# A bidirectional encoder layer: the delta rule's block inverses issued at two places of a recurrence step instead of four

## The chip, the cores and the metric

The kernel runs on one core of one Trainium2 chip. The time is device microseconds of one launch. "Before" was run three times; the figure compared is the median. One further execution was recorded by the hardware profiler, and the profile comes from that one.

## What is computed

One layer of a hybrid encoder: 2048 tokens of width 1024, batch 1. Three branches read the same normalised input through one projection: grouped-query attention, a bidirectional gated delta rule, and cross-attention into 256 memory tokens. Their joint output is gated by silu(z), projected, normalised and added to the input. The change concerns the delta rule alone. The reference, cut to it:

```
lower = jnp.where(strict, jnp.einsum('...id,...jd->...ij', k_beta, k) * decay, 0.0)
t_mat = lower + jnp.eye(CHUNK, dtype=lower.dtype)
rhs = jnp.concatenate([v * beta[..., None], k_beta * jnp.exp(g)[..., None]], axis=-1)
sol = lax.linalg.triangular_solve(t_mat, rhs, left_side=True, lower=True, unit_diagonal=True)
u, w = sol[..., :dv], sol[..., dv:]
...
def step(state, inp):
    qc, kc, uc, wc, ac, dc = inp
    v_new = uc - jnp.einsum('...cd,...de->...ce', wc, state)
    o = jnp.einsum('...cd,...de->...ce', qc, state) + jnp.einsum('...ij,...je->...ie', ac, v_new)
    state = state * dc[..., None, None] + jnp.einsum('...cd,...ce->...de', kc, v_new)
    return state, o
```

It runs forward and backward over the sequence for four heads, and the two directions are summed. The chunk length is free for the kernel to choose, since the recurrence gives the same result for any.

## The kernel before

The layer runs in stages: norms and projections, attention queries and keys, the delta rule's short convolution, the preparation of its chunk matrices, the recurrence (`step`, about 900 to 1262 us of the profile), attention, and the output product. In the profile most instructions stand under line 51, where a helper records every operation, so they are told apart by their tiles.

**The recurrence.** The kernel uses chunks of 128 tokens. One call of `step` treats one chunk of both directions (d) for a pair of heads (h), so each product is four 128x128 float32 matmuls; in the profile these are eight, and every tile below holds all four. There are 16 steps for each of the two head pairs (hp), 32 in all. In a step:

- the scaling of k by the decay to the chunk's end, on VectorE (line 1012: `xx<-xx,tail`)
- `ks`: k times the state St (line 1016); VectorE then makes v minus it, in place in `xx` (line 1018)
- `qp`: q times the state (line 1025); ScalarE scales it into `oo` (line 1027)
- `tx`: F, the inverse of the chunk's triangular matrix, times that difference (line 1032); VectorE scales it into `vn` (line 1035)
- `kv`: the scaled k times vn (line 1043), added to the state by VectorE (line 1048)
- `av`: the chunk's own matrix times vn (line 1053), added into `oo`, which goes to memory (lines 1055 and 1063).

From the ninth step of a pair on, `oo` is added to the other direction's result on GpSimd and squared on ScalarE (lines 1065 to 1072).

**The inverse.** `inverse(hp, s)` is a Python generator that builds F for one chunk and stops after each of its pieces. Each `next` issues one:

1. the loads `nt` (in the profile `n<-NI`) and `ft` (inverses of the 32-row diagonal blocks), and ScalarE's copies of `ft` into F and T
2. `zz` (profile: `invz`), 32x32 matmuls, and ScalarE's copy `zs`
3. `to` and `fo` (`invt`, `invf`), 32x32 matmuls, VectorE's copies into T and ScalarE's into F
4. `z2` (`invy`), 64x64 matmuls, and ScalarE's copy `z2s`
5. `f2` (`inv`), 64x64 matmuls, copied into F by ScalarE (line 995) and VectorE (line 996).

A step is given three generators: `inv` of its own chunk, `inv1` of the next, `inv2` of the one after. Piece 1 of `inv2` is issued just ahead of the step (line 1114). In the running loop the step of chunk n then issued piece 4 of n+1 ahead of `tx` (line 1028), piece 2 of n+2 after it (line 1037), piece 5 of n+1 ahead of `av` (line 1050) and piece 3 of n+2 after it (line 1059). The call at line 1019 found `inv` finished, except in the first step.

**Gate products as fill.** `fill(n)` issues the next n matmuls of work that nobody waits for yet: the projection of the gate z (profile: `z<-hT,wparts`, 128x512, float16, 24 of them to a tile). They stand between the products of the recurrence so that TensorE has something to do while VectorE and ScalarE work. `FILL[4]` to `FILL[10]` say how many at each place of a step. What is not issued there is issued after the recurrence (line 1122).

**Order and buffers.** TensorE is pinned in this stage (line 786): it runs in the order of the text. The other engines and the DMA queues are ordered by a scheduler that works out when each instruction would be ready. An engine's or a queue's order is then fixed, and an instruction that waits holds up those behind it. The loads of this stage go out on SyncE's queue (SP): `nt`, `ft` and `xx` have two buffers each, `it` one. The products that a step takes out of PSUM share four banks under one tag ("tp"), taken in the order of the text: `ks`, `tx`, `kv`, `av` and the five of `inverse`; `qp` and z have four others. F has three buffers, T two; `vn`, `zs` and `z2s` have one each.

During the second pair's steps `side()` issues the end work of the first pair (`finish`), one transpose group (`ot`) in every second step.

Of the kernel before, what the change touches and what calls it, by code (L numbers as in the profile page):

```python
# [30 lines left out]
QW = 256  # L31
START = 3
LAG = 5
FILL = (72, 10, 216, 6, 2, 5, 2, 6, 0, 6, 2, 40, 0, 8)


@with_exitstack
def hybrid_layer(ctx: ExitStack, tc: tile.TileContext, t: dict, out, dbg=None):
# [24 lines left out]
    def dma(to, of):  # L63
        if to.dtype == F32R:
            to, of = to.bitcast(F32), of.bitcast(F32)
        Q.dma_start(to, of)
# [141 lines left out]
    def mm_ps(name, shape=(128, 512)):  # L208
        return mm_pool.tile(list(shape), F32, tag=mm_tag[0], name=name, bufs=mm_tag[1])

    def tp_ps(name, shape=(128, 512)):
        return ps1.tile(list(shape), F32, tag="tp", name=name, bufs=4)
# [565 lines left out]
    def fill(n):  # L778

        for _ in range(n):  # L780
            filled[0] += 1
            next(fill_units, None)
# [4 lines left out]

    fill(FILL[0])
    def bulk(name):
        return bp.tile([128, 2, 4, TB], F32, tag=name, name=name)  # L790
# [12 lines left out]
    with tc.tile_pool(name="s3g", bufs=1, side="right") as p:  # L803
# [48 lines left out]

        fill(FILL[11])
        gp = p.tile([128, 8, 3, 32], F32, tag="gp", name="gp")
# [9 lines left out]
        for i in range(2):  # L864
# [3 lines left out]
            A.copy(grow[:, i], pr[0:96])  # L868
        fill(FILL[12])
        V.tensor_tensor(tail, psg[:, 1], ngc, op=ALU.add)  # L870
# [7 lines left out]
    with tc.tile_pool(name="s3a", bufs=1) as sv0:  # L878
        p = rows
        for hp in range(2):  # L880
            for c in range(TB):
# [18 lines left out]
                dma(NI_d[hp, :, c].rearrange("d p n h i -> p d (n h i)"), ni.rearrange("p d n h i -> p d (n h i)"))  # L900
                fill(FILL[1])
        pr_pool.close()
        sv1 = pr_pool.enter_context(tc.tile_pool(name="s3c", bufs=1, side="right"))
        for hp in range(2):
# [20 lines left out]
            for d, ft in enumerate(((rr, ni), (ni, rr))):  # L925
                for n in range(2):
                    for b in range(4):
                        o = 64 * d + 16 * b
                        dma(FT_d[2 * hp:2 * hp + 2, d, n, :, b].rearrange("h c j i -> c h (j i)"), ft[n][o:o + 16].rearrange("c h j i -> c h (j i)"))
            fill(FILL[2])  # L930
        pr_pool.close()


    with tc.tile_pool(name="s3b", bufs=1) as p:
# [63 lines left out]
        def step(hp, s, St, oss, inv, inv1, inv2, side):  # L998

            nm = f"{hp}_{s}"  # L1000
            cc = (s, TB - 1 - s)
            sh = [128, 2, 2, 128]
            F = Fb[(hp * TB + s) % 3]
            xx = p.tile([128, 2, 4, 2, 128], F32, tag="xx", name=f"xx{nm}", bufs=2)
            it = p.tile(sh, F32, tag="it", name=f"it{nm}")
            kT, qT, kk, vv = (xx[:, :, i] for i in range(4))
            for d in range(2):
                dma(xx[:, d], bx_d[hp, cc[d]])
                dma(it[:, d], NI_d[hp, d, cc[d], :, 1])
            each = [(d, h, 2 * hp + h, cc[d]) for d in range(2) for h in range(2)]  # L1010
            for d, h, hh, c in each:
                V.tensor_scalar(kk[:, d, h, :], kk[:, d, h, :], tail[:, d, hh, c:c + 1], None, op0=ALU.mult)
            if s > 0:
                ks = tp_ps(f"ks{nm}", sh)
                for d, h, hh, c in each:
                    T.matmul(ks[:, d, h, :], kT[:, d, h, :], St[:, d, h, :], start=True, stop=True)
                for d, h, hh, c in each:
                    V.scalar_tensor_tensor(vv[:, d, h, :], ks[:, d, h, :], ngam[:, d, hh, c:c + 1], vv[:, d, h, :], op0=ALU.mult, op1=ALU.add)
            next(inv, None)
            fill(FILL[4])  # L1020
            oo = p.tile(sh, F32, tag="oo", name=f"oo{nm}", bufs=2)
            if s > 0:
                qp = mm_ps(f"qp{nm}", sh)
                for d, h, hh, c in each:
                    T.matmul(qp[:, d, h, :], qT[:, d, h, :], St[:, d, h, :], start=True, stop=True)
                for d, h, hh, c in each:
                    A.activation(oo[:, d, h, :], qp[:, d, h, :], AF.Copy, scale=gam[:, d, hh, c:c + 1])
            next(inv1, None)
            fill(FILL[5])
            tx = tp_ps(f"tx{nm}", sh)  # L1030
            for d, h, hh, c in each:
                T.matmul(tx[:, d, h, :], F[:, d, h, :], vv[:, d, h, :], start=True, stop=True)
            vn = p.tile(sh, F32, tag="vn", name=f"vn{nm}")
            for d in range(2):
                V.tensor_tensor(vn[:, d], tx[:, d], beta[:, d, 2 * hp:2 * hp + 2, cc[d]].unsqueeze(2).to_broadcast([128, 2, 128]), op=ALU.mult)
            fill(FILL[6])
            next(inv2, None)
            side()
            fill(FILL[7])
            if s < TB - 1:  # L1040
                kv = tp_ps(f"kv{nm}", sh)
                for d, h, hh, c in each:
                    T.matmul(kv[:, d, h, :], kk[:, d, h, :], vn[:, d, h, :], start=True, stop=True)
                if s == 0:
                    V.tensor_copy(St, kv)
                else:
                    for d, h, hh, c in each:
                        V.scalar_tensor_tensor(St[:, d, h, :], St[:, d, h, :], egl[:, d, hh, c:c + 1], kv[:, d, h, :], op0=ALU.mult, op1=ALU.add)
            fill(FILL[8])
            next(inv1, None)  # L1050
            av = tp_ps(f"av{nm}", sh)
            for d, h, hh, c in each:
                T.matmul(av[:, d, h, :], it[:, d, h, :], vn[:, d, h, :], start=True, stop=True)
            if s > 0:
                V.tensor_tensor(oo, oo, av, op=ALU.add)
            else:
                A.copy(oo, av)
            fill(FILL[9])
            next(inv2, None)
            fill(FILL[10])  # L1060
            if s < TB // 2:
                for d in range(2):
                    dma(O_d[0][hp, cc[d]], oo[:, d])
                return
            oi = p.tile(sh, F32, tag="oi", name=f"oi{nm}")
            for d in range(2):
                dma(oi[:, d], O_d[0][hp, cc[d]])
            G.tensor_tensor(oo, oo, oi, op=ALU.add)
            for d, h, hh, c in each:
                A.activation(oi[:, d, h, :], oo[:, d, h, :], AF.Square, accum_out=oss[:, h, c:c + 1])  # L1070
            for d in range(2):
                dma(O_d[1][hp, cc[d]], oo[:, d])
# [30 lines left out]
            next(invs[n])  # L1103
        fill(30)
        for k in range(3):
            for n in range(2 if k < 2 else 1):
                next(invs[n])
            fill(FILL[3])
        invs += [iter(()), iter(())]
        for n, (hp, s) in enumerate(order):  # L1110
            if s == 0:
                St = p.tile([128, 2, 2, 128], F32, tag="St", name=f"St{hp}")
                oss = p.tile([128, 2, TB], F32, tag="oss", name=f"oss{hp}", bufs=2)
            next(invs[n + 2], None)
            step(hp, s, St, oss, *invs[n:n + 3], lambda: next(done, None))
            if s == TB - 1:
                done = finish(hp, oss)
# [283 lines left out]
    for i in range(len(blocks) + LAG + 1):  # L1401
# [27 lines left out]
        for tb in range(2):  # L1429
            n = i - len(blocks) - 2 * tb - LAG + 4  # L1430
# [146 lines left out]
```

## Time and profile before

| what | value |
|---|---|
| median of 3 runs | 2406.45 us (2404.51 to 2410.85) |
| profiled execution | 2407.9 us, span 2405.8 us |
| granted TensorE clock, mean | 0.993 |
| DMA over the span | 471.58 MB, mean 196 GB/s |
| recurrence, 900 to 1262 us | 32 steps |

The span goes from the first to the last instruction. In the lines of the profile a time is in us from the span's start, followed by the duration of the run of like instructions, the engine, the operation, `out<-in` by the program's names, the shape and the count. PE is TensorE's matmul, PEld its weight load, DVE VectorE, ACT ScalarE, POOL GpSimd, SPq the queue of SyncE that issues loads. A bracket at the end gives the idle time of the engine just before, and what ended it. Starts of matmuls are measured and their ends modelled, so distances between starts say more than durations. In the table of waits a line has who waited, for whom, the sum in us, how often, and the longest.

### The profile page before, as it was taken

To read this page: it belongs to the slowest core of one execution; us is meant where nothing else is said; L and a number is where in the kernel's file an instruction comes from. 1 tells how busy PE (TensorE), PEld (TensorE's weight loads), DVE (VectorE), ACT (ScalarE), POOL (GpSimd) and SP (SyncE) were. 2 spreads that over 40 slices of the span, in tenths; PEclk is the share of its full clock that TensorE was granted. 3 is DMA by queue.
4 is the path that set the end of the run, shared out by engine and by line. 5 is a ranking of instruction groups with operands and counts; after the bars stand their busy time and mean duration, and the time that the engine had idled before them with its cause. 6 is when DMAs were issued, how large, how long until landed. Compare 5 with 4: busy or idle time off the path is not lost. (4 is left out here: it accounts for less than half of the span.)

```text
span 2405.8 us, 42213 instructions
## 1 busy us (share of the span) xinstructions
PE 2308.4 (96%) x15846; PEld 1463.4 (61%) x15846; DVE 1652.5 (69%) x3338; ACT 1297.4 (54%) x2508; POOL 717.7 (30%) x431
## 2 busy tenths in 40 slices
PE   6999999999999989999999999999999999999998
PEld 6888874455554437667674566666666666544443
DVE  7777558899867855555553778777888877355553
ACT  5633436644443145555554888888888788211110
POOL 2146431111210231020121544445444445122110
PEclk9999999999999999999999999999999999999999
DMA  6446555434377476677765999999999999775551
GB/s 229 141 126 146 133 117 171 125 111 127 113 245 253 107 205 206 203 245 218 242 221 197 243 247 240 242 244 239 239 248 244 243 241 228 217 246 186 175 184 53
DMA packets 942124, 471.58 MB, mean 196 GB/s; under 512 B 721952, under 2 KB 889440, under 8 KB 941664
## 3 DMA queue, kind: packets, MB, share of 16 engines
q1 hardware_dynamic: 929472, 425.88, 69.4%
q0 software_dynamic: 12448, 43.00, 5.3%
q8 instruction: 125, 2.05, 0.4%
q14 instruction: 79, 0.65, 0.1%
HBM read 207.59 MB, written 108.10 MB: 131 GB/s over the span
## 5 line engine op out<-in xcount | busy, mean ns | idle before, releaser
L51 PEld LDWEIGHTS <-wparts 128*128 128x128 f16 x3072 | 293.1, 98 | 317.4 <-issue 6.2
L51 POOL TENSOR_TENSOR hla<-Pa,hla 128x1281 f16<-128x1281 f32 x128 | 335.8, 2624 | 343.2 <-DVE hla L51 320.1
L51 DVE TENSOR_REDUCE mxa<-sa 128x1 f32<-128x1024 f32 x256 | 313.2, 1223 | 130.5 <-PE sa L51 128.6
L51 PE MATMUL sa<-K,qa 128*128 128x512 f16 x1536 | 373.0, 379 | 20.7 <-ACT Pa L51 10.0
L51 PE MATMUL z<-hT,wparts 128*128 128x512 f16 x1536 | 374.0, 381 | 5.4 <-POOL wparts L51 4.7
L51 PE MATMUL pva<-PT,V 128*128 128x256 f16 x3072 | 376.4, 273 | 0.0
L51 ACT ACTIVATE Pa<-sa,mxa,misc 128x1024 f32<-128x1024 f32 x256 | 305.8, 1198 | 95.9 <-POOL hla L51 81.2
L51 PEld LDWEIGHTS <-V 128*128 128x128 f16 x3072 | 300.6, 98 | 84.9
L51 PE MATMUL o<-wo,mhl 128*128 128x512 f16 x1416 | 308.0, 380 | 5.6 <-ACT mhl L51 3.4
L51 PE MATMUL b<-hT,wparts 128*128 128x512 f16 x1152 | 257.8, 380 | 0.0
L51 PEld LDWEIGHTS <-mhl 128*128 128x128 f16 x1464 | 143.5, 98 | 179.9 <-ACT mhl L51 3.7
L51 PEld LDWEIGHTS <-hT 128*128 128x128 f16 x2304 | 226.5, 99 | 40.5 <-issue 4.8
L51 ACT CAST hla<-Pa 128x2048 f16<-128x2048 f32 x128 | 243.0, 1898 | 4.3 <-DMA PT<-hla 0.2
L51 PEld LDWEIGHTS <-qa 128*128 128x128 f16 x1536 | 150.0, 98 | 156.2 <-issue 25.8
L51 PE MATMUL q<-wparts,hT 128*128 128x256 f16 x1920 | 215.0, 276 | 8.5 <-DVE t L51 8.4
L51 POOL TENSOR_SCALAR wraw<-wraw,wsc 128x1024 f32<-128x1024 f32 (+1 forms) x22 | 77.3, 3514 | 278.6 <-DVE wy L51 222.9
L77 POOL DMA_DIRECT2D gate<-zg x64 | 35.5, 554 | 415.1 <-DVE zg L51 284.1
L51 ACT CAST mhl<-mr 128x2048 f16<-128x2048 f32 (+1 forms) x16 | 29.1, 1818 | 221.8 <-PE o L51 173.3
L51 DVE SCALAR_TENSOR_TENSOR y<-xb,convw,y 128x512 f32<-128x512 f32 x192 | 145.9, 772 | 2.0
L51 POOL TENSOR_TENSOR mg<-mg 128x1536 f32<-128x1536 f32 (+1 forms) x16 | 54.9, 3431 | 236.6 <-DMA mg<-r 168.3
L51 DVE SCALAR_TENSOR_TENSOR hla<-Pa,hla 128x768 f16<-128x768 f32 x128 | 121.7, 951 | 0.0
L51 DVE TENSOR_TENSOR mhl<-mr,mhl 128x2048 f16<-128x2048 f32 (+1 forms) x16 | 45.2, 2827 | 90.1 <-ACT mhl L51 90.1
(356 smaller groups left out, 3185.6 us busy)
## 6 DMA issues: line engine op xcount, KB each, us to landing
xx<-bx SPq DMA_DIRECT2D x64, 512.0 KB, 5.9
wraw<-in_w_in POOLq DMA_DIRECT2D x42, 512.0 KB, 5.3
wor<-in_w_out SPq DMA_DIRECT2D x32, 512.0 KB, 4.2
gate<-zg POOLq DMA_DIRECT2D x64, 256.0 KB, 3.7
NI<-nit SPq DMA_DIRECT2D x32, 512.0 KB, 3.0
mr<-mix SPq DMA_DIRECT2D x13, 1024.0 KB, 6.0
mg<-r SPq DMA_DIRECT2D x13, 768.0 KB
x<-in_x SPq DMA_DIRECT2D x16, 512.0 KB
```

The costliest lines, as they stand in the source:

```text
L51: ins = f(*args, **kw)
L77: nc.gpsimd.dma_start(to, of)
```

## The change

Within a step the pieces of the inverses stand at two places. Ahead of `tx`: piece 5 of the step's own inverse and piece 3 of the next one's. Between `kv` and `av`: piece 4 of the next one's and piece 2 of the one after. So the call of `inv` moves from ahead of `qp` to behind it, and those of `inv2` from after `tx` and after `av` to between `kv` and `av`; the last piece of an inverse is now issued in the step that uses F, and each piece has the same place in every step. Ahead of the loop the second inverse is advanced by one piece fewer. One gate product moves from after `tx` (FILL[7], 6 to 5) to ahead of it (FILL[5], 5 to 6).

```
-FILL = (72, 10, 216, 6, 2, 5, 2, 6, 0, 6, 2, 40, 0, 8)
+FILL = (72, 10, 216, 6, 2, 6, 2, 5, 0, 6, 2, 40, 0, 8)
...
-            next(inv, None)
             fill(FILL[4])
             oo = p.tile(sh, F32, tag="oo", name=f"oo{nm}", bufs=2)
...
                     A.activation(oo[:, d, h, :], qp[:, d, h, :], AF.Copy, scale=gam[:, d, hh, c:c + 1])
+            next(inv, None)
             next(inv1, None)
             fill(FILL[5])
             tx = tp_ps(f"tx{nm}", sh)
...
             fill(FILL[6])
-            next(inv2, None)
             side()
             fill(FILL[7])
...
             fill(FILL[8])
             next(inv1, None)
+            next(inv2, None)
             av = tp_ps(f"av{nm}", sh)
...
             fill(FILL[9])
-            next(inv2, None)
             fill(FILL[10])
...
         for k in range(3):
-            for n in range(2 if k < 2 else 1):
+            for n in range(1 if k else 2):
                 next(invs[n])
             fill(FILL[3])
```

More of the change, by code (lines that the diff above doesn't have):

```diff
@@ L33 @@
 LAG = 5
-FILL = (72, 10, 216, 6, 2, 5, 2, 6, 0, 6, 2, 40, 0, 8)
+FILL = (72, 10, 216, 6, 2, 6, 2, 5, 0, 6, 2, 40, 0, 8)
 @with_exitstack
@@ L1018, in step @@
                     V.scalar_tensor_tensor(vv[:, d, h, :], ks[:, d, h, :], ngam[:, d, hh, c:c + 1], vv[:, d, h, :], op0=ALU.mult, op1=ALU.add)
-            next(inv, None)
             fill(FILL[4])
@@ L1027, in step @@
                     A.activation(oo[:, d, h, :], qp[:, d, h, :], AF.Copy, scale=gam[:, d, hh, c:c + 1])
+            next(inv, None)
             next(inv1, None)
@@ L1036, in step @@
             fill(FILL[6])
-            next(inv2, None)
             side()
@@ L1050, in step @@
             next(inv1, None)
+            next(inv2, None)
             av = tp_ps(f"av{nm}", sh)
@@ L1058, in step @@
             fill(FILL[9])
-            next(inv2, None)
             fill(FILL[10])
@@ L1105, in hybrid_layer @@
         for k in range(3):
-            for n in range(2 if k < 2 else 1):
+            for n in range(1 if k else 2):
                 next(invs[n])
```

## The prediction, made before the change was run

> **What bounds the kernel now.** I read the page first, then TensorE's timeline through one recurrence step without a wait, then the table of waits between the first and last step, and only then the other engines around the places where TensorE did wait.
>
> ```profile
> span 2405.8 us, 42213 instructions
> PE 2308.4 (96%) x15846; PEld 1463.4 (61%) x15846; DVE 1652.5 (69%) x3338; ACT 1297.4 (54%) x2508; POOL 717.7 (30%) x431
> ```
>
> TensorE (PE) is busy 96% of the span, so the kernel is as long as TensorE's list of work plus its waits. The change adds and drops no matmul (FILL[4] to FILL[10] sum to 23 gate products a step before and after), so it can act in two ways only: fewer changes between kinds of matmul, and fewer or longer waits. After the recurrence the list goes on gate products and attention with the same 96%, so I pass on a gain or a loss one to one. The step from 1011.73 to 1022.96 is a quiet one:
>
> ```profile
> 1011.73 1.05 PE L51 MATMUL ks<-St,xx 128*128 128x128 f32 x8
> 1012.62 0.59 PE L51 MATMUL z<-hT,wparts 128*128 128x512 f16 x2
> 1013.05 1.05 PE L51 MATMUL qp<-St,xx 128*128 128x128 f32 x8
> 1014.03 0.45 PE L51 MATMUL invy<-T,n 64*64 64x64 f32 x8
> 1014.41 1.25 PE L51 MATMUL z<-hT,wparts 128*128 128x512 f16 x5
> 1015.50 1.05 PE L51 MATMUL tx<-xx,F 128*128 128x128 f32 x8
> 1016.39 0.59 PE L51 MATMUL z<-hT,wparts 128*128 128x512 f16 x2
> 1016.92 0.33 PE L51 MATMUL invz<-ft,n 32*32 32x32 f32 x16
> 1017.18 1.47 PE L51 MATMUL z<-hT,wparts 128*128 128x512 f16 x6
> 1018.49 1.05 PE L51 MATMUL kv<-vn,xx 128*128 128x128 f32 x8
> 1019.47 0.45 PE L51 MATMUL inv<-F,z2s 64*64 64x64 f32 x8
> 1019.85 1.16 PE L51 MATMUL av<-vn,it 128*128 128x128 f32 x8
> 1020.84 1.46 PE L51 MATMUL z<-hT,wparts 128*128 128x512 f16 x6
> 1022.23 0.22 PE L51 MATMUL invt<-zs,F 32*32 32x32 f32 x2
> ...
> 1022.52 0.61 PE L51 MATMUL z<-hT,wparts 128*128 128x512 f16 x2
> 1022.96 1.05 PE L51 MATMUL ks<-St,xx 128*128 128x128 f32 x8
> ```
>
> The durations overlap, so I go by the distance from one start to the next. The step takes 11.23 us. Its four small groups are invy (0.38 us), invz (0.26), inv (0.38) and invt with invf (0.29).
>
> ```profile
> 907.73 1.05 PE L51 MATMUL ks<-St,xx 128*128 128x128 f32 x8
> ```
>
> ```profile
> 1256.75 1.05 PE L51 MATMUL ks<-St,xx 128*128 128x128 f32 x8
> ```
>
> ```profile
> 1169.50 0.66 PE L51 MATMUL ot<-ident,fi 128*128 128x128 f32 x4
> 1169.99 1.46 PE L51 MATMUL z<-hT,wparts 128*128 128x512 f16 x6
> ```
>
> From the first ks (907.73, step 1) to the last (1256.75, step 31) there are 349.0 us and 30 steps. Thirty quiet steps are 336.9. Seven of them carry four transposes ot at 0.49 (1169.50 to 1169.99), 3.4 more. At the change of head pair the last step has no kv and the first no ks and qp, 0.98 + 0.89 + 0.98 = 2.85 less. That makes 337.5, so **11.5 us are waits**, the most that better cover could win inside the loop. The table of waits says who waits:
>
> ```profile
> DVE xx L51 <- DMA xx<-bx: 75.9, 43, 4.6
> PEld tx L51 <- DVE xx L51: 6.6, 11, 1.1
> PE invy L51 <- DVE T L51: 4.0, 4, 1.8
> ```
>
> Both TensorE waits have one root, seen in one step near 1165:
>
> ```profile
> 1165.09 0.29 DVE L51 TENSOR_SCALAR xx<-xx,tail 128x128 f32<-128x128 f32 x1 [3.68 <-DMA xx<-bx]
> 1165.40 0.47 DVE L51 COPY T<-invt 32x64 f32<-32x64 f32 x2
> ```
>
> ```profile
> 1165.67 0.69 PE L51 MATMUL invy<-T,n 64*64 64x64 f32 x8 [0.68 <-DVE T L51]
> ```
>
> VectorE (DVE) has the *next* step's tail scaling (xx<-xx,tail, line 1012) ahead of this step's T copies and of v minus ks (line 1018, the DVE xx that tx waits for). It stands 3.68 us for the next load of xx, and invy and then tx wait behind it. What releases that load is on SP's queue:
>
> ```profile
> 1014.57 0.86 SPq L51 DMA_DIRECT2D n<-NI  x2
> 1017.31 1.91 SPq L51 DMA_DIRECT2D ft<-FT  x4
> 1019.57 0.81 SPq L51 DMA_DIRECT2D xx<-bx  x2
> ```
>
> n goes out when invy has freed its buffer (1014.41), ft when invz has (1017.18), xx when kv has (1019.47). Each load follows the matmul that frees its room, not the text.
>
> **The new step.** By line 1019 and after, it is ks, 2 z, qp, [inv of this step, invt and invf of the next], 6 z, tx, 2 z, 5 z, kv, [invy of the next, invz of the one after], av, 8 z. The gate products last 0.216 us each (five from 1014.41 to 1015.50, with rounding).
>
> *Changes of kind.* Two z ahead of ks take 0.43 to 0.44 us (1012.62 to 1013.05), the two ahead of invz 0.53 (1016.39 to 1016.92): entering a small group costs 0.09. qp lasts 0.98 ahead of invy where ks ahead of z lasts 0.89: again 0.09. Of four such entries two go, 0.18 us x 31 steps = 5.6 us at most; but the 64-row group now meets the 32-row one inside each place, which no row of before shows. The nearest row is the entry after a float32 product, 0.09, by which nothing is gained. The ends are 5.6 gained and, if leaving invz for av is dearer than leaving inv (0.99 instead of 0.89 for av), 1.5 lost. I take 1.0 gained, near that row. The Trainium skill, "TensorEngine Tiling (Array Packing)", Tiling Modes, says that a change of tiling mode, not of tile, drains TensorE. The entries of 0.09 agree with it; by it the inner change is paid too, and the sum would be 1.0 us worse.
>
> *The waits at invy go.* T is written after invt and read by invy. Between them lie now 2 z, ks, 2 z, qp: 2.7 us. After the change it is 6 z, tx, 7 z, kv: 1.30 + 0.89 + 1.51 + 0.98 = 4.7 us. But VectorE's hold-up by the load stays, and tx stands behind the same instruction. From the end of ks to tx it was 0.43 + 0.98 + 0.38 + 1.09 = 2.88 us and becomes 0.43 + 0.98 + 0.38 + 0.29 + 1.30 = 3.38: the moved z and the moved invt group together give 0.5 us more. Against it, tx needs a new thing, below. With the load landing as now, the waits would mostly move from invy to tx.
>
> *The load of xx.* In SP's queue n and ft stand ahead of xx, 4 ft issues of 1.91 us in all. Now invy and invz come after kv, so n is freed 0.38 us and ft 0.64 us after kv's end, and xx, freed at kv's end, should go out first. The order is the scheduler's choice; I read it from the three rows above, where order is release order. xx's transfer then shares its first microsecond with no ft. The ft issues ended (1019.22) 0.35 us before xx. I estimate xx to land 0.6 us sooner, between 0 and 1.5: 11 waiting steps (the row of PEld tx) x 0.6 = 6.6 us gained, with 0 and 11.5 as ends. n and ft go out up to 5 us later, and have until the second place of the step after, over 11 us; I cost that at nothing.
>
> *The new wait at tx.* inv now runs in the same step as tx, and F (its copies on ACT and DVE) must be ready.
>
> ```profile
> 1014.14 1.14 ACT L51 ACTIVATE oo<-qp,gam 128x128 f32<-128x128 f32 x4 [0.48 <-PE qp L51]
> 1019.96 0.26 ACT L51 COPY F<-inv 64x128 f32<-64x128 f32 x1 [1.19 <-PE inv L51]
> 1190.58 1.13 ACT L51 ACTIVATE oo<-qp,gam 128x128 f32<-128x128 f32 x4
> ```
>
> ```profile
> 1188.32 1.05 PE L51 MATMUL qp<-St,xx 128*128 128x128 f32 x8
> ```
>
> ScalarE (ACT) scales qp into oo first: from 0.11 us after qp (1014.03) to 1.25 after it. F's copy then ends at 1.51. tx begins 0.38 + 0.29 + 1.30 = 1.97 after qp. So 0.4 us remain in a quiet step, and the wait costs nothing; the cover is the six z and the invt group. The T<-ft copies, which sit behind oo now, wait for invy and so move behind the second place. Where ACT is late there is no cover: with qp over at 1189.30 oo ends at 1191.71, F at 1191.97, while tx would start at 1191.27: 0.7 us. I saw only a few such steps, and this one waits for xx anyway. On VectorE F's other copy, about as long, stands behind v minus ks, and only the second half of tx reads it, 0.45 us later. I charge 1.2 us, between 0 and 16 (0.5 us in every step, if ACT has other work ahead of F).
>
> *kv after tx.* vn needs 0.8 us after tx, and now 2 z, invz and 6 z cover it (2.10 us from 1016.39 to 1018.49). After the change 7 z are 1.51. Quiet steps keep 0.5; steps whose vn stands behind a late xx lose up to 0.6. I charge 0.9, between 0 and 3.
>
> *The start of the loop.*
>
> ```profile
> 892.19 0.22 PE L51 MATMUL invt<-zs,F 32*32 32x32 f32 x2 [1.16 <-ACT zs L51]
> 897.76 0.45 PE L51 MATMUL inv<-F,z2s 64*64 64x64 f32 x8 [2.04 <-ACT z2s L51]
> 894.83 1.22 ACT L51 COPY F<-ft 32x128 f32<-32x128 f32 x4 [2.03 <-DMA ft<-FT]
> ```
>
> Line 1105 now advances the second inverse once instead of twice, so the wait of 1.16 has no place. The second wait hangs on ACT, which stood for ft until 894.83; TensorE comes to inv sooner and meets the same landing. I take 1.0 gained, between 0 and 3.2.
>
> **Sum.** Gained 1.0 + 6.6 + 1.0, lost 1.2 + 0.9: 6.5 us less. The profiled execution took 2407.9 us, 2.1 more than its span of 2405.8; less 6.5 that is 2401.4. The median of the runs, 2406.45, is 1.45 below it, so I forecast **2400.0 us**. A measurement of this kernel tells about 0.3% (7.2 us) from no change, so the likeliest result lies just inside "the same".
>
> **The rivals.**
>
> *All waits go.* If xx lands over a microsecond sooner and the inner changes of kind cost nothing, 11.5 + 5.6 + 1.0 less 2.1 makes 16 us: 2390. For it speaks the one root of both waits; against it, xx has waited up to 4.6 us in that view, much more than ft can account for. Chance 0.14.
>
> *The waits change place only.* xx lands as now, the T copies no longer hold up invy, but v minus ks and F's copy hold up tx, and kv has less cover: 1.0 + 1.0 - 2.1, about nothing, 2406.5. For it speaks that v minus ks stands behind the same load in the same queue. Chance 0.14.
>
> *Slower: xx behind n and ft.* If SP's order keeps n and ft ahead of xx, their release now comes after kv: xx would go out 0.64 us plus 1.91 of ft issues, some 2.5 us later. A step has at most about 1.3 us of slack to give (0.5 of it the new cover ahead of tx), so 1.2 us x 31 = 37: 2444. It decides from about 1.3 us of delay on. Against it stands that each load goes out when freed. The lesser form, F late at tx in every step, would give up to 16 us. Together 0.12.
>
> **How the numbers follow.** The forecast's case has 0.60. It runs from about 1 to 12 us less, so a little under half of it (0.27) is beyond 7.2. Faster: 0.27 + 0.14 = 0.41; the same: 0.33 + 0.14 = 0.47; slower: 0.12. The range goes from 2392, which takes in most of the first rival, to 2409, the second rival with the larger prices for tx and kv; the slower one stays out.
>
> **What would show it.** Right: on SP, xx directly behind kv with n and ft after it; the wait of DVE xx for DMA xx well under 75.9 us; no wait of invy for T; quiet steps of 11.1 to 11.2 us; tx waiting for F in a few steps only. Wrong: tx waiting for ACT F in most steps, or kv for vn; SP holding xx behind ft; quiet steps near 11.0, which would mean that the inner changes are free.

## The result, and the profile after

The changed kernel takes **2432.64 us** (median of 6 runs, 2430.93 to 2437.5), beside 2411.61 us for the kernel before (6 runs, 2404.51 to 2413.78; the three of the table above are among them). The ratio is **1.0087** (95% interval 1.0072 to 1.0103): slower by 0.9%, where 2400.0 us and "just inside the same" were forecast. The profiled execution took 2437.5 us, the longest of the six, so its distance to the profile of before (29.9 us of span) is larger than that of the medians (21.0 us).

The page of the changed kernel begins:

```profile
span 2435.7 us, 42288 instructions
PE 2314.2 (95%) x15838; PEld 1472.1 (60%) x15846; DVE 1647.6 (68%) x3338; ACT 1293.5 (53%) x2508; POOL 719.5 (30%) x431
```

TensorE's list of work is the same and its busy time grew by 6 us; the mean granted clock was 0.987 here and 0.993 before. The first and the last ks of the loop, from its timeline, say where:

```profile
903.26 1.05 PE L51 MATMUL ks<-St,xx 128*128 128x128 f32 x8
```

```profile
1278.06 1.05 PE L51 MATMUL ks<-St,xx 128*128 128x128 f32 x8
```

That is 374.8 us for what took 349.0: 25.8 us more.

**The quiet step is better than forecast.** TensorE's timeline through one step without a wait:

```profile
998.61 0.45 PE L51 MATMUL invy<-T,n 64*64 64x64 f32 x8
998.98 0.33 PE L51 MATMUL invz<-ft,n 32*32 32x32 f32 x16
999.24 1.16 PE L51 MATMUL av<-vn,it 128*128 128x128 f32 x8
1000.24 1.89 PE L51 MATMUL z<-hT,wparts 128*128 128x512 f16 x8
...
1003.28 1.05 PE L51 MATMUL qp<-St,xx 128*128 128x128 f32 x8
1004.27 0.45 PE L51 MATMUL inv<-F,z2s 64*64 64x64 f32 x8
...
1004.93 1.47 PE L51 MATMUL z<-hT,wparts 128*128 128x512 f16 x6
...
1008.64 1.05 PE L51 MATMUL kv<-vn,xx 128*128 128x128 f32 x8
1009.62 0.45 PE L51 MATMUL invy<-T,n 64*64 64x64 f32 x8
...
1010.26 1.16 PE L51 MATMUL av<-vn,it 128*128 128x128 f32 x8
```

From av to av it takes 11.02 us; before it took 11.23. invy ahead of invz takes 0.37 to 0.38 us, invz ahead of av 0.26, and inv with the 32-row group behind it 0.66 (1004.27 to 1004.93). These are the lengths that the four groups had when each stood alone (0.38, 0.26, 0.38 + 0.29). Thirty-one times 0.21 us is 6.5 us gained. With allowances as in the prediction (seven times the transposes, which take 0.44 here, where they took 0.49, and 2.85 for the change of pair), thirty quiet steps make 330.8 us. So about **44 us** of the loop are something else than quiet steps, where 11.5 were.

**The waits.** From the table of waits over the recurrence (who waits for whom: us in all, times, longest):

```profile
PE kv L51 <- DVE vn L51: 11.5, 9, 3.0
PE tx L51 <- ACT F L51: 7.3, 8, 2.3
PE av L51 <- DVE ga L51: 4.1, 3, 2.3
PE tx L51 <- DVE F L51: 1.6, 2, 1.3
DVE xx L51 <- DMA xx<-bx: 110.6, 52, 5.4
```

invy waits for T no more. But kv waits for vn, tx waits for F, and VectorE's wait for the load of xx went from 75.9 to 110.6 us. TensorE's four rows hold 24.5 us, a good half of the 44. (av waits for `ga`, VectorE's reading of the transposes `ot`: in the compiled program av has the PSUM bank of `ot` in the seven steps that have one. Run 1, below, where the load is in its place, has no such wait, and runs 2 and 4, where it is late, have it; so the late load seems to be behind it too.)

**The load of xx.** SP's queue around one kv of the changed kernel, and that kv from TensorE's timeline:

```profile
927.27 1.05 PE L51 MATMUL kv<-vn,xx 128*128 128x128 f32 x8
```

```profile
928.36 0.33 SPq L51 DMA_DIRECT2D xx<-bx  x1
928.79 0.85 SPq L51 DMA_DIRECT2D n<-NI  x2
...
930.21 0.42 SPq L51 DMA_DIRECT2D it<-NI  x1
930.84 0.79 SPq L51 DMA_DIRECT2D Od<-oo  x2
...
932.20 1.48 SPq L51 DMA_DIRECT2D ft<-FT  x3
933.72 0.47 SPq L51 DMA_DIRECT2D xx<-bx  x1
```

Before, both halves of xx (one for each direction) stood together behind kv ("xx<-bx x2" at 1019.57 in the prediction's rows). Now the first half still goes out at kv's end. The second goes out 5.4 us later, behind the loads of n, ft and it and behind the stores of oo. That is one of the shorter delays: in the first pair's steps the second half leaves 5.4 to 9.1 us after kv's end. What follows from it, on VectorE and then TensorE, one step on:

```profile
938.23 0.48 DVE L51 TENSOR_SCALAR xx<-xx,tail 128x128 f32<-128x128 f32 x2 [0.77 <-DMA xx<-bx]
938.62 0.75 DVE L51 TENSOR_TENSOR vn<-tx,beta 128x256 f32<-128x256 f32 x2
```

```profile
939.10 1.16 PE L51 MATMUL kv<-vn,xx 128*128 128x128 f32 x8 [0.64 <-DVE vn L51]
```

The tail scaling of the late half stands ahead of vn in VectorE's fixed order. It waits for the load, vn waits behind it, and kv waits for vn.

**F.** One of the steps in which tx waits for F, with rows of ScalarE, TensorE and VectorE in order of time:

```profile
1051.61 0.45 PE L51 MATMUL inv<-F,z2s 64*64 64x64 f32 x8
1052.30 0.31 ACT L51 ACTIVATE oi<-oo 128x128 f32<-128x128 f32 x1 [1.38 <-POOL oo L51]
...
1053.49 1.11 ACT L51 ACTIVATE oo<-qp,gam 128x128 f32<-128x128 f32 x4
1054.48 0.25 ACT L51 COPY F<-inv 64x128 f32<-64x128 f32 x1
...
1054.79 0.71 PE L51 MATMUL tx<-xx,F 128*128 128x128 f32 x4 [1.05 <-ACT F L51]
1055.97 0.48 DVE L51 TENSOR_SCALAR xx<-xx,tail 128x128 f32<-128x128 f32 x2 [3.18 <-DMA xx<-bx]
1056.48 0.29 DVE L51 COPY F<-inv 64x128 f32<-64x128 f32 x1
1056.83 1.22 PE L51 MATMUL tx<-xx,F 128*128 128x128 f32 x4 [1.33 <-DVE F L51]
```

inv itself is in time, at 1051.61. ScalarE stands 1.38 us for GpSimd's sum, because the squares of the *previous* step's output are ahead in its order. Then come the squares, then oo, and only then F's copy. F's other half, on VectorE, stands behind a tail scaling that waits 3.18 us for its load. So tx waits twice in one step.

**The clock.** A second price hangs on the waits. A step in which tx waits for F, from TensorE's timeline, and the windows around it (busy time and count for each engine, then the granted clock, the DMA share and GB/s):

```profile
1090.74 2.07 PE L51 MATMUL tx<-xx,F 128*128 128x128 f32 x8 [2.29 <-ACT F L51]
...
1094.76 1.05 PE L51 MATMUL kv<-vn,xx 128*128 128x128 f32 x8
```

```profile
1088.00:1090.00 2.00, 0.45 (x3) 0.00 (x0) 1.94 (x4) 0.74 (x5) 1.23 (x1) 1.00 0.70 199
1090.50:1093.50 3.00, 2.76 (x11) 2.15 (x12) 2.07 (x9) 2.67 (x11) 0.00 (x0) 0.50 0.32 83
...
905.00:1280.00 375.00, 347.17 (x3566) 250.30 (x3565) 191.65 (x618) 194.42 (x751) 58.29 (x56) 0.97 0.69 210
```

After 2.29 us of standing still TensorE's clock is at half, and tx takes 2.07 us instead of 1.05. In windows of 0.5 us the half clock lasts 3.0 to 3.4 us here, and the kv behind it has its 1.05 us again. In windows of 1 us I find five such stretches in the loop (from 913, 1056, 1090, 1135 and 1186 us), the first twice as long. Each begins at or just behind (at 1134.9, 1.3 us behind) a wait of 2.3 to 3.0 us, or, at 1056, the two of 1.05 and 1.33 close together that the rows of F show. What the clock lacks of 1.00 adds up to 10.2 us. The last row says the same for the whole loop: 0.97 over 375 us, where the loop of before has 1.00 throughout. So of the 44 us about 25 are waits and 10 are work at half the clock behind them. Three smaller rows of TensorE hold 3.4 us more, and about 6 us are in no row. The Trainium skill, "TensorE: Matmul & The Clock Gate", Why this matters for your kernels, advises to keep gaps under about 3 us for this reason; here 2.3 us were enough, so its figure is too wide for this trace. Not each such wait does it: run 1, below, has one of 2.46 us and keeps its clock, and run 2 has a stretch behind a wait of 1.5 us.

### The profile page after: what moved, and what is told of

Read it like the earlier page. It is cut to its first block, busy times and chain, and to the rows that moved or that the text cites. A ratio compares the mean times of both kernels' runs of the same rounds, so it can differ in the third digit from the quotient of the medians.

```text
span 2435.7 us, 42288 instructions
## 1 busy us (share of the span) xinstructions
PE 2314.2 (95%) x15838; PEld 1472.1 (60%) x15846; DVE 1647.6 (68%) x3338; ACT 1293.5 (53%) x2508; POOL 719.5 (30%) x431
## 4 chain that ended last, share of the span: by engine, by line
PE 34%; DMA 6%; issue 5%; POOL 4%; DVE 3%; ACT 2%; SPq 1%; POOLq 0%; DVEq 0%; ACTq 0%
PE o L51 12%; PE sa L51 8%; PE pva L51 8%; POOL hla L51 3%; PE z L51 2%; DMA PT<-hla 2%; DMA xx<-bx 1%; SPq L51 1%; DMA wor<-in_w_out 1%; PE sm L51 1%; DVE mxm L51 1%; PE pvm L51 1%; PE av L51 1%; ACT Pa L51 1%; DVE mxa L51 0%
## 5 line engine op out<-in xcount | busy, mean ns | idle before, releaser
L51 PEld LDWEIGHTS <-wparts 128*128 128x128 f16 x3072 | 299.0, 99 | 329.9 <-issue 11.6
L51 PE MATMUL z<-hT,wparts 128*128 128x512 f16 x1536 | 369.1, 384 | 5.6 <-POOL wparts L51 4.7
L51 DVE TENSOR_SCALAR xx<-xx,tail 128x128 f32<-128x128 f32 x128 | 37.5, 333 | 110.9 <-DMA xx<-bx 110.6
```

What stands on the lines that cost most here:

```text
L51: ins = f(*args, **kw)
```

## The experiments

Two theories stood after this reading. **A, the order of the loads:** the second half of xx goes out 5 us late, because invy and invz now free n and ft just behind kv, and everything that comes earlier in the text goes first once it is free. **B, F too late:** the last piece of an inverse now runs in the step that uses F, behind whatever ScalarE and VectorE have queued. The ratios are to the kernel before, timed beside each kernel on the same chip, with their 95% intervals; the medians of before lay between 2411.2 and 2413.6 us. Diffs are against the changed kernel where nothing else is said.

**1. The loads of xx written first.** They are written one step earlier in the text, ahead of the inverse's loads; no matmul moves.

```
-                dma(xx[:, d], bx_d[hp, cc[d]])
...
+            for x in order[n:n + 2] if n == 0 else order[n + 1:n + 2]:
+                load_xx(*x)
```

> The changed kernel with one edit: the two loads of xx are written one step earlier in the text, ahead of the inverse's loads, so that both halves go out together as soon as kv has freed the buffer. TensorE's order stays that of the changed kernel. Theory A (the loads): the second half of xx stands on SP behind n, ft, it and the stores of oo, goes out some 5 us after kv instead of 0.4, and VectorE, which stands for it, holds up vn and so kv. Then this edit takes the waits of kv for vn (11.5 us in the changed kernel) to under 3 us, and the ratio to the kernel before falls from 1.009 to about 1.002 or less. Theory B (late F): the inverse's last piece now ends in the step that uses it, and tx waits for ScalarE's copy of F. Then the waits of tx stay at 7 us or more, and the ratio stays at 1.006 or above.

2412.37 us, ratio **1.0012** (0.9999 to 1.0026). Some 18 of the 21 us are gone (0.75% of 2411), and the granted clock is 1.00 over the loop. SP's queue and the kv ahead of it:

```profile
929.81 1.05 PE L51 MATMUL kv<-vn,xx 128*128 128x128 f32 x8
```

```profile
930.89 0.81 SPq L51 DMA_DIRECT2D xx<-bx  x2
931.80 0.85 SPq L51 DMA_DIRECT2D n<-NI  x2
```

Both halves go out behind kv again, n after them. In TensorE's rows of the table of waits kv is gone:

```profile
PE tx L51 <- DVE xx L51: 7.0, 7, 2.5
PE tx L51 <- ACT F L51: 1.8, 4, 0.7
PE tx L51 <- DVE F L51: 1.6, 3, 0.8
```

The waits of tx for F fell as well, from 8.9 to 3.4 us: part of F's lateness was the late load in another place. Theory A carries the main cost. But the kernel is now only as fast as before, although its quiet steps are 11.02 us. Something still eats the 6.5 us.

**2. F early.** The last piece is issued behind av and FILL[9], one step ahead, as a third place.

```
+            next(inv1, None)
```

> The changed kernel with one edit: the last piece of the next step's inverse (inv) is issued behind av of the step ahead, with the 2 gate products of FILL[10] after it, so that F is ready long before tx; SP's order stays the changed kernel's, with the second half of xx behind ft. Theory A (the loads) expects the waits of kv for vn to stay at about 10 us and the ratio to stay at 1.005 or above. Theory B (late F) expects the waits of tx for F (8.9 us on TensorE) to vanish and the ratio to fall to 1.004 or less.

2430.22 us, ratio 1.0087 (1.0068 to 1.0106): nothing gained. The wait of tx for F is gone from TensorE's rows, and kv's wait for vn grew from 11.5 to 14.4 us; the clock is at half in four stretches (6.8 us lost), one of them behind a wait of 1.47 us (kv at 952.41). The third place makes the quiet steps 11.12 us. As long as the load is late, an earlier F only moves the wait from tx to kv. So theory B is not the main cause; whether it costs anything by itself this run can't say.

**3. Each inverse half a step earlier.** There are two places again, invy and invz ahead of tx, and inv with invt and invf ahead of av. That frees n and ft before kv and has F ready early. Ahead of the loop the inverses are advanced as in the kernel before, and the call ahead of FILL[4] has work in the first step only.

```
+            next(inv, None)
...
-            next(inv, None)
             next(inv1, None)
+            next(inv2, None)
```

> Two places as in the changed kernel, but each inverse half a step earlier: ahead of tx its second piece (invz) and the next one's fourth (invy), ahead of av the last piece (inv) and the third (invt, invf). n and ft are then freed at the first place, far from kv, and F is ready half a step before tx. Quiet steps should last 11.02 us as in the changed kernel, against 11.23. Both theories expect the waits to fall back to the 11.5 us of the kernel before or below, and so a ratio of about 0.997. If instead the two places themselves cost (64-row groups next to 32-row ones, or less cover ahead of kv), it stays above 1.003.

2432.12 us, ratio 1.0089 (1.0072 to 1.0105). The loads were in order (VectorE's wait for xx 40.5 us) and no wait of tx for F was left, and still it was as slow as the change. A new wait had come in nearly every step. TensorE and ScalarE:

```profile
1014.36 0.85 ACT L51 COPY F<-invf 32x64 f32<-32x64 f32 x4
```

```profile
1012.48 1.05 PE L51 MATMUL kv<-vn,xx 128*128 128x128 f32 x8
...
1015.26 1.16 PE L51 MATMUL av<-vn,it 128*128 128x128 f32 x8 [1.06 <-ACT F L51]
```

av begins when ScalarE's copies of invf end (1015.21), in the table 20.1 us in 19 steps, and 5.2 us more for VectorE's St. Yet av reads only vn and `it`. What it can share with those copies is a PSUM bank: kv, inv, invt, invf and av are five products in a row, and the tag has four banks. The compiled program of this run agrees: the bank of av was last invf's in 19 of the 32 steps, as many as wait for ScalarE's F, and kv's, which St reads, in 10. (So the four banks are not taken strictly in turn.) Runs 5 and 9 test that.

**4. The gate product moved back.** FILL[5] and FILL[7] as before, the rest as changed.

```
-FILL = (72, 10, 216, 6, 2, 6, 2, 5, 0, 6, 2, 40, 0, 8)
+FILL = (72, 10, 216, 6, 2, 5, 2, 6, 0, 6, 2, 40, 0, 8)
```

> The changed kernel with the one gate product back behind tx (FILL[5] 5, FILL[7] 6). It gives kv 0.216 us more cover and tx as much less. Theory A expects kv's waits (9 of them) to lose some 2 us, theory B expects tx's waits (8) to gain as much: a ratio of 1.007 to 1.010 in both. If the product that was moved away from kv were the cause, the ratio would fall to 1.003 or less.

2437.74 us, ratio 1.011 (1.0086 to 1.0134). That is a little above the 1.007 to 1.010 expected, but the interval overlaps that of the change; if anything the moved product helps by 0.2%. It is not the cause.

**5. Half a step earlier, the second place behind av.** As run 3, with inv, invt and invf moved from ahead of av to behind it (the diff is against run 3).

```
-            next(inv1, None)
-            next(inv2, None)
...
+            next(inv1, None)
+            next(inv2, None)
```

In this order the first place issues piece 4 of the next inverse and piece 2 of the one after, the second pieces 5 and 3.

> The two places again half a step earlier for each inverse, but the second place stands behind av instead of ahead of it (invy and invz ahead of tx; inv, invt and invf behind av). Loads n and ft are freed ahead of tx, so SP sends xx right behind kv as in the kernel before, and F is ready half a step early. Theory A (the order of the loads made the change slow; two places in themselves are worth the quiet step, 11.02 instead of 11.23): quiet steps 11.0 to 11.1, no wait of kv for vn over 3 us in sum, no wait of tx for F, no wait of av for F; ratio to before about 0.996 (0.994 to 0.999). Rival B (two places leave too little work between the products, wherever they stand): waits of 25 us and more in the loop, ratio 1.003 or more. If the wait of av in the run before this one came from ScalarE's copies as such and not from av's place behind the small products, ks will wait instead, about 1 us in each step: ratio 1.009.

2398.65 us, ratio **0.9955** (0.9939 to 0.9972): faster than both kernels. The first and the last ks of its loop, and the waits of tx and of kv's weight loads that are left:

```profile
907.14 1.05 PE L51 MATMUL ks<-St,xx 128*128 128x128 f32 x8
```

```profile
1242.71 1.05 PE L51 MATMUL ks<-St,xx 128*128 128x128 f32 x8
```

```profile
PE tx L51 <- DVE xx L51: 2.3, 4, 0.8
PEld kv L51 <- DVE vn L51: 2.9, 7, 0.5
```

The loop takes 335.6 us, 13.4 less than before. av waits no more, and ks doesn't wait in its place. The quickest steps are 10.93 us, even 0.09 less than in the changed kernel: kv is now followed by av and takes 0.89 us, not 0.98, while av takes 0.98 ahead of the small group, and took 1.00 behind it. But six steps of the first pair take 11.17 or 11.18, because kv's weights wait there for vn, which stands on VectorE behind work on a gate product. Two places in themselves are a gain.

**6. The change with its second place behind av.** F is as late as in the change, but n and ft come free after av.

```
-            next(inv1, None)
-            next(inv2, None)
...
+            next(inv1, None)
+            next(inv2, None)
```

> The changed kernel with its second place (invy of the next inverse, invz of the one after) behind av instead of ahead of it; the last piece of an inverse still runs in the step that uses F. On SP n and ft now wait for a point behind av, and in the order of the queue both halves of xx stand together. Theory A (load order): kv waits for vn under 3 us in sum, ratio to before 1.000 (0.998 to 1.003), as with the loads of xx written first. Theory B (F is ready too late when its last piece runs in the same step): tx still waits for F 15 us or more and the ratio stays at 1.006 to 1.009.

2405.81 us, ratio **0.9976** (0.9963 to 0.999). Moving two small groups past one product is worth 1.1% against the change. On SP both halves of xx go out behind kv, no wait of kv is left on TensorE, and the clock is whole. What is left in the table is B:

```profile
PEld tx L51 <- ACT F L51: 7.3, 9, 2.4
PEld tx L51 <- DVE F L51: 6.1, 13, 1.5
PE tx L51 <- DVE xx L51: 4.9, 5, 1.9
```

Runs 5 and 6 have the same places, and their quickest steps the same 10.93 us. They differ in whether F's last piece runs a half step ahead of tx's step or in it, and with that in which pieces stand at which place. That difference is 0.21%, 5 us by the ratios and 7.2 us by the medians, which were taken together on one chip.

**7. The control: the loads of xx written first in the kernel before.** The edit of run 1, made to the kernel before.

> The kernel before, with the loads of xx written one step earlier in the text, ahead of the inverse's loads, as in the first experiment; the inverse stays at four places. Theory A (that edit helped the changed kernel only because it gives xx back its place in the queue): here both halves of xx already go out right behind kv, so nothing changes, ratio 1.000 (0.998 to 1.002). Rival (loads written earlier help any of these kernels, so the first experiment shows nothing of the change): ratio about 0.992, as between the changed kernel and the first experiment.

2410.28 us, ratio 0.9995 (0.9981 to 1.0009). Where the loads already go out together the edit does nothing. So run 1 gained by undoing a damage of the change, not by an improvement of its own.

**8. The gate product alone, in the kernel before** (the diff is against that kernel).

```
-FILL = (72, 10, 216, 6, 2, 5, 2, 6, 0, 6, 2, 40, 0, 8)
+FILL = (72, 10, 216, 6, 2, 6, 2, 5, 0, 6, 2, 40, 0, 8)
```

> The kernel before with the gate product moved ahead of tx alone; the inverse stays at four places. With moving it back in the changed kernel at 1.011 beside 1.009, I expect the move to be worth 0 to 5 us: about 0.2 us more cover for tx in the 11 steps in which it waits for xx (2 us), 0.2 us less for kv, which had 0.5 us to spare. Ratio 0.998 to 1.000. If the moved product takes kv's cover in the steps with a late xx, ratio 1.001 to 1.002.

2410.71 us, ratio 0.9998 (0.9985 to 1.0011): no difference. In its profile TensorE's clock is at half once, from 1162 us, behind a wait of kv for vn of 2.51 us.

**9. Run 3 with another bank for av** (against run 3).

```
-            av = tp_ps(f"av{nm}", sh)
+            av = mm_ps(f"av{nm}", sh)
```

> The kernel in which each inverse is half a step earlier and the second place stands ahead of av (the third experiment), with one edit: av takes its PSUM bank from the four of qp and z instead of the four that it shares with ks, tx, kv and the inverse. If av waited there for a bank that ScalarE's copies of invf still held, the wait of av for ScalarE's F (20 us) and for VectorE's St (5 us) goes, quiet steps come to about 11.0, and the ratio to the kernel before is about 0.996 (0.994 to 1.000), as with the second place behind av. If av waited for the copies for another reason, the waits stay and the ratio is about 1.009. If the z products now run out of banks, a wait of z shows and the ratio lies between.

2406.11 us, ratio 0.9968 (0.9954 to 0.9983), against 1.0089 for run 3. av's waits are gone from the table, and the loop falls from 366.8 to 340.1 us. It was the bank. (kv's weights wait here and there for vn, as in run 5.)

**10. Both edits, 1 and 2, in the changed kernel.**

> The changed kernel with both edits: the loads of xx written ahead of the inverse's loads (first experiment) and the last piece of each inverse issued behind av a step ahead, so that F is early (second experiment). Alone the first came to 1.0012 and the second to 1.0087, as the change itself. If F's lateness is a cost of its own that the late load of xx hides (kv and tx wait for whichever comes last), taking it away shows now: no wait of tx for F, ratio 0.996 to 0.998. If F's lateness costs nothing, the ratio stays at 1.001, or a little above by the third place (about 0.1 us in each step).

2407.29 us, ratio **0.9979** (0.9967 to 0.9991), against 1.0012 without the early F. With the load in its place, an early F is worth 0.33%, some 8 us, where it was worth nothing in run 2. Runs 1, 2, 10 and the change make a square: the late load hides the late F, because tx and kv wait for whichever comes last.

## Why the prediction was wrong

**The step that failed** is "The load of xx": "xx, freed at kv's end, should go out first. The order is the scheduler's choice; I read it from the three rows above, where order is release order." Those rows could not tell release order from another rule, since in them n, ft and xx came free microseconds apart. The change brought the three releases to within 0.64 us, and there the order of the text decided: the first half of xx went out, and then n, ft and `it`, written earlier, passed the second. Even `it` and the stores of oo, also written earlier, went ahead of it, though they came free only 1.6 and 2.5 us after kv's end (av over at 929.89, oo at 930.78, kv at 928.26). Run 1 shows it by moving nothing but the text, run 6 by moving the releases apart again. Instead of 6.6 us gained the term was about 18 lost (run 1 against the change, with F late in both; 26 by the ratios of runs 10 and 2, with F early in both), work at half the clock included. How the scheduler weighs readiness against the text I infer from these orders; it is not shown further.

The third rival, "xx behind n and ft", had this mechanism, and 2444 as its price. I gave it most of 0.12 for the reason that "each load goes out when freed", the same misreading. It priced the whole xx as 2.5 us late and paid 1.2 us in every step. In fact half of xx goes out 5.4 us late and more, and it costs where VectorE stands behind it, nothing in a quiet step and up to 3 us in a bad one, with the half clock behind the longest waits, which no part of the prediction had.

**The other terms:**

| term of the sum | forecast, us | measured, us | from |
|---|---|---|---|
| changes of kind | 1.0 gained | 6.5 gained | quiet step 11.23 to 11.02, 31 times |
| xx sooner, waits of invy and tx | 6.6 gained | about 18 lost | run 1 against the change |
| tx waits for F | 1.2 lost (0 to 16) | 5 to 8 lost | runs 6 against 5, 10 against 1 |
| kv's cover | 0.9 lost (0 to 3) | 0 to 3 lost | waits of kv's weights for vn: 0.7 in run 1, 0.2 in run 6, 2.9 in run 5 |
| start of the loop | 1.0 gained | 1.1 gained | below |
| sum | 6.5 gained | 15 to 21 lost | the medians say 21.0 lost |

- *Changes of kind.* The upper end of the range was right, and a little more. By the rule of the Trainium skill ("TensorEngine Tiling (Array Packing)", Tiling Modes) the passage from 64-row to 32-row matmuls would drain TensorE. No row here shows a price for it: invy ahead of invz takes 0.37 to 0.38 us, as ahead of a gate product. The 0.09 of an entry is paid once a place, after the 128-row product (qp 0.99, kv 0.98), and about as much at av behind invz (1.00, where tx ahead of gate products takes 0.89), as it was behind inv before (0.99). The measurement decides.
- *F.* The quiet step's 0.4 us of spare time held: quiet steps lose nothing. Too small was the share of steps in which ScalarE is late. I saw "only a few such steps" before. But in that kernel F's last piece ran half a step earlier, so ScalarE's queue ahead of F could not show as a wait.
- *kv's cover.* Seven gate products are enough in most steps, and fell short in some steps of run 5 by about 0.25 us. What kv waited for in the changed kernel was mainly the load, through VectorE.
- *The start.* From the first invz to the first ks the kernel before took 18.95 us (907.73 less 888.78) and the changed one takes 17.89 (903.26 less 885.37):

```profile
888.78 0.57 PE L51 MATMUL invz<-ft,n 32*32 32x32 f32 x32
```

```profile
885.37 0.57 PE L51 MATMUL invz<-ft,n 32*32 32x32 f32 x32
```

The signs I named for "wrong" were kv waiting for vn, SP holding xx behind ft, tx waiting for F, and quiet steps near 11.0. All four came, tx's wait in 8 to 10 steps and not in most. Of the signs for "right", invy's wait for T did go.

## What to carry to other kernels

When a change moves the points at which buffers come free, write out the new releases of every load on the queue. Where several fall within the time that the queue takes to issue them, don't assume release order: assume that what stands earlier in the text goes first, and put the load that is needed first there, or keep its release apart from the others. A wait that vanishes after an edit isn't yet a gain: the late F cost nothing while the load was later, and 5 to 8 us once it was not. Waits on TensorE of some 1.5 us and more are to be priced with the clock that they may cost. And where more products stand in a row than their tag has PSUM banks, one of them gets a bank that another engine may still be reading; moving the group to behind the next large product made the order of run 3 0.45% faster than before, in place of 0.89% slower.

## What the hardware did that I had not expected

The clock, above all: TensorE standing still for 2.3 us can be enough to halve it for the next 3 us or so, and then the wait costs about 1.6 us more than itself. The length of the wait alone doesn't decide it. In the loops of all the kernels here, each of the four waits of over 2.5 us had such a stretch at it or behind it (2.51, 2.67, 2.86 and 2.97), but of those from 1.4 to 2.46 us only some (1.47 in run 2 did, 2.45 in run 4 and 2.46 in run 1 didn't). What decides between these the runs don't show. The kernel before and runs 1, 5, 6, 7, 9 and 10 have no such stretch, run 8 one.

A run of small matmuls pays 0.09 us once, at its entry from a 128-row product, nothing between its 64-row and its 32-row parts, and about 0.1 us more where a float32 product follows it and not a gate product. And a product whose operands were ready stood 1.06 us in a step for a PSUM bank that another engine was still copying out of; the table of waits names ScalarE's F there, which the product doesn't read. With a bank of the other tag (run 9) the wait was gone, and the kernel took 1.2% less.
